# A first group's convolution ahead of the split and GpSimd work, the output projection's last weights in the decays' tiles, and Sqrt in a second norm

## The chip, the cores and the metric

The kernel runs on one core of a Trainium2 chip. The metric is the device time of one execution in microseconds. The program is one launch; three runs of the kernel before gave 746.96, 748.88 and 749.24 us, with a median of 748.88 us.

The core's engines are named as in the profile: PE (TensorE: matmuls and transposes), DVE (VectorE), ACT (ScalarE), POOL (GpSimd) and SP (SyncE, which issues the DMAs here). Each takes its own instructions in order; across engines they wait on semaphores.

## The reference

One sequence of 512 tokens with 1024 features goes through two layers and a norm, all in float32.

```python
def mamba2_layer(x, ...):
    h = rms_norm(x, norm_g)
    zxbcdt = h @ w_in
    # split into z, xbc, dt_raw
    xbc = silu(causal_depthwise_conv(xbc, conv_w, conv_b))      # 4 taps
    # xbc -> xs (heads), bm, cm (8 groups);  dt = softplus(...), a = -exp(a_log)
    y = ssd_chunked_scan(xs * dt[..., None], a * dt, bm, cm)
    y = y + d_skip * xs
    y = gated_group_rms_norm(y, z, gate_norm_g)                # norm of y * silu(z) per group
    return x + y @ w_out
...
x = mamba2_layer(x, ...)
k, v = shared_kv(x, kv_norm_g, w_kv)                           # own rms_norm, then x @ w_kv
x = diff_attention_layer(x, k, v, ...)                         # own rms_norm, queries and gate
return rms_norm(x, final_norm_g)
```

In the scan, with acs the running sum of a * dt within a chunk, position l sees position s of its chunk through exp(acs[l] - acs[s]) where s <= l and through zero elsewhere. This matrix is called the decay below. The two norms behind the first layer (for keys and values, and for the attention layer) divide by the same root, so the kernel computes it once; it is the second norm of the title. The sums of squares of a row's two halves go into it.

## The kernel before, in words

**Products.** Each float32 product is made of three matmuls (`mm3`): both factors are split into a rounded part and the rest, and hi*hi, hi*lo and lo*hi are summed. So each megabyte of weights (a segment) arrives by one DMA in a tile `raw`, and is split there by two operations for each slice k: `head` on ACT writes `whi`, `rest` on DVE writes `wlo` (`load`, `lay`). `raw`, `whi` and `wlo` have two buffers each. `use(seg)` fetches two segments ahead of the one that is used, and lays all pieces of a fetched segment in one go (`fetch`). From the last output projection on, `use_b` does it instead, and `paced` hands out the pieces one by one between the matmuls; `later(n, fn)` puts work off by n steps of that clock.

**The Mamba layer.** It has 8 groups, g0 to g7. The order of segments is written out by hand: z0 g0 g1 z1 g2 g3 z2 g4 o0 g5 z3 g6 g7 o1 o2 o3, each of two segments ("g",1,1 is the second one of g1, "o",3,1 the last one of the output projection), then v0 and the attention's. `group_proj(g)` projects into four PSUM banks pg and calls `conv` on each: u (DVE), Identity with the last tap (ACT), three taps by SCALAR_TENSOR_TENSOR (DVE), Silu (ACT). The results xc are B, C, x0 and x1 of the group. `z_proj` makes the gates zs by Silu from its banks pz, which are of the same four as pg.

`ssd(g)` is the scan of a group: pcb = B*C on PE, transposes pbt and pxt of B and x, xdt and dx from pxt (DVE), xe from xdt (POOL), dec * pcb (DVE), the states hst (psA, psB on PE, products on POOL, sums on DVE), pyd = dec times xdt on PE, po = C times the states, tmp from po; then gating, squares on ACT, a root on DVE (`rsqrt`, eight operations for one value), tmp scaled on ACT, its transposes pyt on PE, and yh and yl from these, which the output projection multiplies.

`decays(j)` (lines 497 to 515) makes the decay of groups 2j and 2j+1: a DMA brings acs into `dec` on all partitions (two buffers, so the DMA waits until the matmuls pyd of two groups before have read theirs), POOL copies `een` out, subtracts (TENSOR_TENSOR, four heads) and masks (AFFINE_SELECT), and ACT takes Exp of een and of dec in two halves. Exp and Silu each make ACT load another table (ACT_TABLE_LOAD), when the other was there before. `decays(0)` is called ahead of the groups, the next ones in `ssd` of g1, g3 and g5.

**Order.** Up to `last_rows` (line 637) a scheduler of the compiler sets the order of each engine. From `T.on = V.on = A.on = True` on, the order is that in which the program is written. All operations of DVE, ACT and PE go through the helper `Ordered` and so have its line, L53; the tiles tell them apart.

**The end of the Mamba layer.** `last_rows` multiplies by o31 (the weights of "o",3,1) and calls `row_norm(t, po)` for each of four blocks t of 128 tokens: after 1 step the add into x_tok (DVE), after 3 the square with its sum (ACT), after 6 the root (DVE: b_v, then seven operations of `rsqrt`), after 4 more the Copy with that scale into xn (ACT). `turn_rows` transposes xn (btp on PE) for the projections behind. Meanwhile v0's pieces are laid, one per two steps.

Of the kernel before, what the change touches and what calls it, by code (L numbers as in the profile page):

```python
# [9 lines left out]
F32 = mybir.dt.float32  # L10
F32R = mybir.dt.float32r
# [50 lines left out]
def trunk(ctx, tc, x, x_t, par, w_dt, w_in, w_out, w_kvqg, w_bo, d_skip, lam_qk, fin_g, out):  # L62
# [58 lines left out]
    def load(i):  # L121
# [8 lines left out]
        def split():  # L130
            hi = wp.tile([P, nk, w], F32R, tag="whi", name=f"whi{i}", bufs=2)
            lo = wp.tile([P, nk, w], F32R, tag="wlo", name=f"wlo{i}", bufs=2)
# [29 lines left out]

    def fetch(upto):
        while fetched[0] < min(upto, len(segs)):
            for piece in load(fetched[0])():
                lay(piece)
# [20 lines left out]
    def use_b(seg, first=None, pace=None):  # L187
# [3 lines left out]
        if i + 2 < len(segs) and fetched[0] == i + 2:  # L191
            loaded[i + 2] = load(i + 2)
        if i + 1 in loaded:
# [25 lines left out]
    def rsqrt(v, n, tag, bufs=2):  # L219
# [20 lines left out]
        return y  # L240

# [72 lines left out]
    conv_out = {}  # L314

# [122 lines left out]
    def conv(ps, ft, name, bufs):  # L438
# [5 lines left out]
        for k in (2, 1, 0):  # L444
            d = 3 - k
            V.scalar_tensor_tensor(out=xc[:, d:], in0=u[:, :S - d], scalar=cw[k], in1=xc[:, d:], op0=ALU.mult, op1=ALU.add)
# [3 lines left out]
    def group_proj(g):  # L450
# [14 lines left out]
        conv_out[g] = outs  # L465

# [30 lines left out]
    def decays(j):  # L497

        for g in (2 * j, 2 * j + 1):
            hs = slice(R * g, R * g + R)  # L500
            dec = bp.tile([P, R, NQ, P], F32, tag="dec", name=f"dec{g}", bufs=2)
            nc.sync.dma_start(dec.rearrange("p h c l -> p (h c l)"),
                                acs_d[hs].rearrange("h c l -> (h c l)").partition_broadcast(P))
            een = small.tile([P, R, 2], F32, tag="een", name=f"een{g}")
            GP.tensor_copy(een, dec[:, :, 1:3, P - 1])
            for h in range(R):
                GP.tensor_tensor(out=dec[:, h], in0=dec[:, h], in1=acs_tok[:, :, R * g + h].unsqueeze(2).to_broadcast([P, NQ, P]), op=ALU.subtract)  # L507
                GP.affine_select(out=dec[:, h], in_=dec[:, h], compare_op=ALU.is_ge, fill=-BIG, base=0,
                                 pattern=[[0, NQ], [1, P]], channel_multiplier=-1)
            decs[g] = (dec, een)  # L510
        for g in (2 * j, 2 * j + 1):
            dec, een = decs[g]
            A.activation(een, een, AF.Exp)
            for h in range(0, R, 2):
                A.activation(dec[:, h:h + 2], dec[:, h:h + 2], AF.Exp)
# [476 lines left out]
```

## Time and profile before

| what | us |
|---|---|
| median of three runs | 748.88 |
| the profiled execution's own time | 747.46 |
| its span, first to last instruction | 745.7 |
| PE busy | 723.1 |
| DVE busy | 553.5 |
| ACT busy | 437.9 |
| POOL busy | 132.3 |
| ACT_TABLE_LOAD, 27 of them | 34.6 |

A row of the timeline has the start in us from the span's beginning, the duration, the engine, the line, the operation, the tiles as output<-inputs, partitions x elements and types, how many like it were merged, and in brackets the idle time of the engine ahead of it with what ended it. The mean granted clock of PE is 0.993.

### The profile page before, as it was taken

What the parts mean: (1) busy time and instruction counts of PE and PEld (TensorE: products, weight loads), DVE (VectorE), ACT (ScalarE), POOL (GpSimd) and SP (SyncE); (2) the same over time, 40 slices, a digit from 0 to 9 for tenths busy, and PEclk for the clock granted to TensorE, in tenths of its full rate; (3) what the DMA queues carried; (4) which work ended last, traced back from release to release, by engine and by line L of the source; (5) the groups of instructions that cost most, each with busy time, mean ns of one, the idle gap of its engine ahead of it and who ended that gap; (6) DMA issues with size and microseconds to landing.
All of it is one profiled execution on the core that took longest, in us unless ns stands there. A gap on an engine that the chain in (4) does not pass through costs nothing.

```text
span 745.7 us, 10346 instructions
## 1 busy us (share of the span) xinstructions
PE 723.1 (97%) x3741; PEld 606.7 (81%) x3741; DVE 553.5 (74%) x1232; ACT 437.9 (59%) x951; POOL 132.3 (18%) x162
## 2 busy tenths in 40 slices
PE   9998999999999999998999998999999999999992
PEld 7786878888888888887888878888988898898881
DVE  5579994799679859667995648557767867885987
ACT  6837763574747428439542357657766766755535
POOL 0109261602515024150210110000000000000004
PEclk9999999999999999999999999999999999999997
DMA  9543223232213332221212111331221131131003
GB/s 317 204 150 136 96 75 114 69 125 89 113 57 113 120 125 74 95 96 62 108 62 109 57 57 65 113 113 57 65 106 56 58 114 57 58 114 57 29 1 113
DMA packets 12914, 70.83 MB, mean 95 GB/s; under 512 B 1600, under 2 KB 2112, under 8 KB 5312
## 3 DMA queue, kind: packets, MB, share of 16 engines
q1 hardware_dynamic: 12576, 70.06, 25.9%
q8 instruction: 29, 0.48, 0.3%
q10 hardware_dynamic: 288, 0.12, 0.1%
q14 instruction: 21, 0.17, 0.1%
HBM read 68.02 MB, written 2.16 MB: 94 GB/s over the span
## 4 chain that ended last, share of the span: by engine, by line
PE 81%; DVE 6%; ACT 5%; issue 4%; DMA 2%; POOL 0%; SPq 0%; ACTq 0%; POOLq 0%; DVEq 0%
PE pg L53 16%; PE po L53 14%; PE pz L53 9%; PE pt L53 7%; PE pq L53 6%; PE pk L53 6%; PE pv L53 6%; PE pb L53 5%; PE pyd L53 4%; PE sc L53 3%; DVE wlo L53 2%; ACT whi L53 1%; DVE xc L53 1%; DMA raw<-in_w_in 1%; PE psA L53 1%
## 5 line engine op out<-in xcount | busy, mean ns | idle before, releaser
L53 DVE SCALAR_TENSOR_TENSOR wlo<-raw,prm,whi 128x512 fp32r<-128x512 f32 (+1 forms) x256 | 155.6, 652 | 47.1 <-ACT whi L53 46.5
L53 ACT ACTIVATE whi<-raw,prm 128x512 fp32r<-128x512 f32 (+1 forms) x256 | 136.9, 604 | 46.0 <-PE po L53 14.4
L53 PE MATMUL pg<-a_hi,whi 128*128 128x512 f32 x256 | 102.8, 403 | 0.0
L53 PE MATMUL pg<-a_lo,whi 128*128 128x512 f32 x256 | 102.7, 401 | 0.0
L53 PE MATMUL pg<-a_hi,wlo 128*128 128x512 f32 x256 | 102.5, 401 | 0.0
L53 DVE SCALAR_TENSOR_TENSOR xc<-u,prm,xc 128x511 f32<-128x511 f32 (+2 forms) x96 | 79.7, 846 | 6.9 <-ACT xc L53 6.4
L53 PEld LDWEIGHTS pg<-a_hi,wlo 128*128 128x128 f32 x256 | 48.1, 188 | 10.9
L53 PEld LDWEIGHTS pg<-a_hi,whi 128*128 128x128 f32 x256 | 48.2, 188 | 10.9
L53 PEld LDWEIGHTS pg<-a_lo,whi 128*128 128x128 f32 x256 | 48.2, 188 | 10.5
L891 POOL TENSOR_TENSOR ot<-x_tok,fg 128x512 f32<-128x512 f32 x8 | 10.0, 1284 | 259.2 <-DVE x_tok L53 258.3
L53 PE MATMUL po<-whi,yh 128*128 128x512 f32 x128 | 51.3, 401 | 0.6 <-ACT yh L53 0.6
L53 PE MATMUL pz<-whi,a_lo 128*128 128x512 f32 x128 | 50.8, 397 | 0.0
L53 PE MATMUL po<-wlo,yh 128*128 128x512 f32 x128 | 50.7, 396 | 0.0
L53 PE MATMUL pz<-wlo,a_hi 128*128 128x512 f32 x128 | 50.6, 395 | 0.0
L53 PE MATMUL po<-whi,yl 128*128 128x512 f32 x128 | 50.3, 397 | 0.0
L53 PE MATMUL pz<-whi,a_hi 128*128 128x512 f32 x128 | 50.2, 404 | 0.0
L53 ACT ACTIVATE xc<-u,prm 128x512 f32<-128x512 f32 x32 | 25.8, 811 | 40.2 <-DVE u L53 40.1
L53 DVE CUSTOM_DVE_ANT_0 s<-sc,bias 128x128 f32<-128x128 f32 (+3 forms) x64 | 29.7, 486 | 22.7 <-PE sc L53 22.4
L545 POOL TENSOR_TENSOR xe<-xdt,tok 128x256 f32<-128x256 f32 x24 | 16.3, 707 | 149.1 <-DVE xdt L53 149.1
L507 POOL TENSOR_TENSOR dec<-dec,tok 128x512 f32<-128x512 f32 x32 | 40.5, 1296 | 0.6
L53 ACT ACT_TABLE_LOAD x27 | 34.6, 1283 | 9.2 <-DVE xc L53 6.3
L53 ACT ACTIVATE tmp<-dx 128x256 f32<-128x256 f32 x32 | 13.2, 412 | 45.1 <-DVE dx L53 45.1
(220 smaller groups left out, 1776.8 us busy)
## 6 DMA issues: line engine op xcount, KB each, us to landing
raw<-in_w_in SPq DMA_DIRECT2D x23, 1024.0 KB, 4.9
raw<-in_w_kvqg SPq DMA_DIRECT2D x16, 1024.0 KB, 4.8
dec<-acs_d SPq DMA_DIRECT2D x8, 1024.0 KB, 4.8
raw<-in_w_out SPq DMA_DIRECT2D x8, 1024.0 KB, 4.8
raw<-in_w_bo SPq DMA_DIRECT2D x4, 1024.0 KB, 4.9
xt<-in_x_t SPq DMA_DIRECT2D x8, 256.0 KB, 6.1
x_tok<-in_x SPq DMA_DIRECT2D x4, 512.0 KB, 8.7
out<-ot SPq DMA_DIRECT2D x8, 256.0 KB, 2.1
```

The lines of the kernel that those rows point to most:

```text
L53: i = op(*args, **kw)
L507: GP.tensor_tensor(out=dec[:, h], in0=dec[:, h], in1=acs_tok[:, :, R * g + h].unsqueeze(2).to_broadcast([P, NQ, P]), op=ALU.subtract)
L545: GP.tensor_tensor(out=xe[:, c], in0=xdt[:, c], in1=toe_tok[:, c, hs].unsqueeze(2).to_broadcast([P, R, HD]), op=ALU.mult)
L891: GP.tensor_tensor(out=ot[t][:, hs], in0=y, in1=fg[:, hs], op=ALU.mult)
```

## The change

There are three edits in one.

1. *First group.* The pieces of ("g",1,1) are held back in a list and laid after g0's convolutions; with `tc.issue_after` they may not stand ahead of the last tap. `decays` is cut into `decay_in` (the DMA), `decay_sub` (POOL) and `decay_exp` (ACT). At the start only group 0's decay is made whole, group 1 has its DMA alone; its subtractions follow POOL's operations of `ssd(0)`, and its Exp is written inside `ssd(0)`. Later decays are called as before, as `decays(g + 1, g + 2)`.
2. *Last weights.* The split of ("o",3,1) writes the two `dec` buffers instead of `whi` and `wlo`, and at `use_b(("o",3,0))` all of v0's pieces are laid at once.
3. *Roots.* `root1` makes a row's root by Sqrt on ACT and four small DVE operations (the negative value, a reciprocal, and one correction step), with other steps for `later`; the third `beside(8)` of the stretch is `beside(16)`.

```diff
         def split():
-            hi = wp.tile([P, nk, w], F32R, tag="whi", name=f"whi{i}", bufs=2)
-            lo = wp.tile([P, nk, w], F32R, tag="wlo", name=f"wlo{i}", bufs=2)
+
+            pool, tags = (bp, ("dec", "dec")) if seg == ("o", 3, 1) else (wp, ("whi", "wlo"))
+            hi, lo = (pool.tile([P, nk, w], F32R, tag=tag, name=f"{n}{i}", bufs=2) for n, tag in zip(("whi", "wlo"), tags))
             ready[seg] = (hi, lo)
...
 
+    held = []
+
     def fetch(upto):
         while fetched[0] < min(upto, len(segs)):
-            for piece in load(fetched[0])():
-                lay(piece)
+            held.extend(load(fetched[0])())
+            if segs[fetched[0] - 1] != ("g", 1, 1):
+                while held:
+                    lay(held.pop(0))
 
...
             loaded[i + 2] = load(i + 2)
+        if seg == ("o", 3, 0):
+            for piece in loaded.pop(i + 2)():
+                lay(piece)
         if i + 1 in loaded:
...
+
+    def root1(ss, vb, k, tag):
+
+        s, y, c, nv = (small.tile([P, 1], F32, tag=f"{tag}_{i}", name=f"{tag}_{i}", bufs=2) for i in "sycn")
+        A.activation(s, ss, AF.Sqrt, scale=k, bias=vb)
+
+        def rest():
+            V.tensor_scalar(out=nv, in0=ss, scalar1=-k, scalar2=vb, op0=ALU.mult, op1=ALU.subtract)
+            V.reciprocal(y, s)
+            V.tensor_scalar(out=c, in0=y, scalar1=nv, scalar2=y, op0=ALU.mult, op1=ALU.mult)
+            V.tensor_scalar(out=y, in0=c, scalar1=3.0, scalar2=y, op0=ALU.add, op1=ALU.mult)
+            return y
+
+        return rest
 
...
             d = 3 - k
-            V.scalar_tensor_tensor(out=xc[:, d:], in0=u[:, :S - d], scalar=cw[k], in1=xc[:, d:], op0=ALU.mult, op1=ALU.add)
+            conv_end[0] = V.scalar_tensor_tensor(out=xc[:, d:], in0=u[:, :S - d], scalar=cw[k], in1=xc[:, d:], op0=ALU.mult, op1=ALU.add)
         A.activation(xc, xc, AF.Silu)
...
 
+        if held:
+            with tc.issue_after(conv_end[0].ins):
+                while held:
+                    lay(held.pop(0))
+
...
 
-    def decays(j):
-
-        for g in (2 * j, 2 * j + 1):
-            hs = slice(R * g, R * g + R)
-            dec = bp.tile([P, R, NQ, P], F32, tag="dec", name=f"dec{g}", bufs=2)
-            nc.sync.dma_start(dec.rearrange("p h c l -> p (h c l)"),
-                                acs_d[hs].rearrange("h c l -> (h c l)").partition_broadcast(P))
-            een = small.tile([P, R, 2], F32, tag="een", name=f"een{g}")
+    def decay_in(g):
+
+        hs = slice(R * g, R * g + R)
+        dec = bp.tile([P, R, NQ, P], F32, tag="dec", name=f"dec{g}", bufs=2)
+        nc.sync.dma_start(dec.rearrange("p h c l -> p (h c l)"),
+                          acs_d[hs].rearrange("h c l -> (h c l)").partition_broadcast(P))
+        decs[g] = (dec, small.tile([P, R, 2], F32, tag="een", name=f"een{g}"))
+
+    def decay_sub(g, heads=range(R)):
+        dec, een = decs[g]
+        if 0 in heads:
             GP.tensor_copy(een, dec[:, :, 1:3, P - 1])
-            for h in range(R):
-                GP.tensor_tensor(out=dec[:, h], in0=dec[:, h], in1=acs_tok[:, :, R * g + h].unsqueeze(2).to_broadcast([P, NQ, P]), op=ALU.subtract)
-                GP.affine_select(out=dec[:, h], in_=dec[:, h], compare_op=ALU.is_ge, fill=-BIG, base=0,
-                                 pattern=[[0, NQ], [1, P]], channel_multiplier=-1)
-            decs[g] = (dec, een)
-        for g in (2 * j, 2 * j + 1):
-            dec, een = decs[g]
-            A.activation(een, een, AF.Exp)
-            for h in range(0, R, 2):
-                A.activation(dec[:, h:h + 2], dec[:, h:h + 2], AF.Exp)
+        for h in heads:
+            GP.tensor_tensor(out=dec[:, h], in0=dec[:, h], in1=acs_tok[:, :, R * g + h].unsqueeze(2).to_broadcast([P, NQ, P]), op=ALU.subtract)
+            GP.affine_select(out=dec[:, h], in_=dec[:, h], compare_op=ALU.is_ge, fill=-BIG, base=0,
+                             pattern=[[0, NQ], [1, P]], channel_multiplier=-1)
+
+    def decay_exp(g):
+        dec, een = decs[g]
+        A.activation(een, een, AF.Exp)
+        for h in range(0, R, 2):
+            A.activation(dec[:, h:h + 2], dec[:, h:h + 2], AF.Exp)
+
+    def decays(*gs):
+        for g in gs:
+            decay_in(g)
+            decay_sub(g)
+        for g in gs:
+            decay_exp(g)
+
+    def behind(g, i, heads):
+        if g == 0:
+            with tc.issue_after(i.ins):
+                decay_sub(1, heads)
 
...
         for c in range(3):
-            GP.tensor_tensor(out=xe[:, c], in0=xdt[:, c], in1=toe_tok[:, c, hs].unsqueeze(2).to_broadcast([P, R, HD]), op=ALU.mult)
+            xe_end = GP.tensor_tensor(out=xe[:, c], in0=xdt[:, c], in1=toe_tok[:, c, hs].unsqueeze(2).to_broadcast([P, R, HD]), op=ALU.mult)
+
+        behind(g, xe_end, (0,))
         for h in range(R):
...
         A.copy(hsf[:, 0], psA[:, 0:256])
-        GP.tensor_tensor(out=hst[:, 1], in0=hst[:, 0], in1=een[:, :, 0:1].to_broadcast([P, R, HD]), op=ALU.mult)
+        i = GP.tensor_tensor(out=hst[:, 1], in0=hst[:, 0], in1=een[:, :, 0:1].to_broadcast([P, R, HD]), op=ALU.mult)
+        behind(g, i, (1,))
         V.tensor_tensor(out=hsf[:, 1], in0=psA[:, 256:512], in1=hsf[:, 1], op=ALU.add)
         psB = ss_bank(f"psB{g}")
         T.matmul(psB[:, 0:256], lhsT=bt[:, 2, :], rhs=xe[:, 2].rearrange("p h e -> p (h e)"), start=True, stop=True)
-        GP.tensor_tensor(out=hst[:, 2], in0=hst[:, 1], in1=een[:, :, 1:2].to_broadcast([P, R, HD]), op=ALU.mult)
+        i = GP.tensor_tensor(out=hst[:, 2], in0=hst[:, 1], in1=een[:, :, 1:2].to_broadcast([P, R, HD]), op=ALU.mult)
+        behind(g, i, (2, 3))
+        if g == 0:
+            decay_exp(1)
         V.tensor_tensor(out=hsf[:, 2], in0=psB[:, 0:256], in1=hsf[:, 2], op=ALU.add)
...
         if g % 2 and g < G - 1:
-            decays((g + 1) // 2)
+            decays(g + 1, g + 2)
 
...
     decays(0)
+    decay_in(1)
     dense[0] = stream_a()
...
-
-        def root():
-            v = small.tile([P, 1], F32, tag="f_v", name=f"b_v{t}", bufs=2)
-            V.scalar_tensor_tensor(out=v, in0=bss[:, 1, t:t + 1], scalar=ROOT2 / D, in1=bss[:, 0, t:t + 1], op0=ALU.mult, op1=ALU.add)
-            r = rsqrt(v, 1, "f")
-            later(4, lambda: A.activation(xn[t], x_tok[:, t], AF.Copy, scale=r))
+            rest = root1(bss[:, 1, t:t + 1], bss[:, 0, t:t + 1], 4.0 / D, "b")
+            later(3, lambda: root(rest))
+
+        def root(rest):
+            r = rest()
+            later(2, lambda: A.activation(xn[t], x_tok[:, t], AF.Copy, scale=r))
 
         later(1, lambda: V.tensor_tensor(out=y, in0=po, in1=y, op=ALU.add))
         later(3, square)
-        later(6, root)
 
...
     T.on = V.on = A.on = True
-    later(9, lambda: V.tensor_scalar(out=bss[:, 0], in0=bss[:, 0], scalar1=ROOT2 / D, scalar2=ROOT2 * EPS, op0=ALU.mult, op1=ALU.add))
+    later(9, lambda: V.tensor_scalar(out=bss[:, 0], in0=bss[:, 0], scalar1=4.0 / D, scalar2=4.0 * EPS, op0=ALU.mult, op1=ALU.add))
     dense[0] = paced(last_rows())
...
     turn_rows("b", 3, xn[3], hh, hl)
-    beside(8)
+    beside(16)
     flush()
```

**Where the orders differ.** The orders of PE, ACT, DVE and POOL differ from g0's convolutions up to about g3 and again from o3 on; in between they are the same, and SP's is the same throughout. ACT has 36 table loads instead of 27.

First DVE at the end of g0's convolutions, before; xc_614 is x0, xc_634 x1, u their scaled input, wlo_553 the second segment of g1, dec_440 group 0's decay:

```order
L53 SCALAR_TENSOR_TENSOR xc_614<-u_615,prm,xc_614 128x511
L53 TENSOR_TENSOR u_635<-pg_3_489,ar_row 128x512
L53 SCALAR_TENSOR_TENSOR wlo_553<-raw_550,prm,whi_552 128x512
L53 SCALAR_TENSOR_TENSOR xc_614<-u_615,prm,xc_614 128x510
L53 SCALAR_TENSOR_TENSOR wlo_553<-raw_550,prm,whi_552 128x512 x3
L53 SCALAR_TENSOR_TENSOR xc_614<-u_615,prm,xc_614 128x509
L53 SCALAR_TENSOR_TENSOR xc_634<-u_635,prm,xc_634 128x511
L53 SCALAR_TENSOR_TENSOR xc_634<-u_635,prm,xc_634 128x510
L53 SCALAR_TENSOR_TENSOR xc_634<-u_635,prm,xc_634 128x509
L53 TENSOR_TENSOR dec_440<-dec_440,pcb_661 128x512 x4
```

The same place now, where the names are xc_586 and xc_606 and wlo_533:

```order
L53 SCALAR_TENSOR_TENSOR xc_586<-u_587,prm,xc_586 128x511
L53 TENSOR_TENSOR u_607<-pg_3_469,ar_row 128x512
L53 SCALAR_TENSOR_TENSOR xc_586<-u_587,prm,xc_586 128x510
L53 SCALAR_TENSOR_TENSOR xc_586<-u_587,prm,xc_586 128x509
L53 SCALAR_TENSOR_TENSOR xc_606<-u_607,prm,xc_606 128x511
L53 SCALAR_TENSOR_TENSOR xc_606<-u_607,prm,xc_606 128x510
L53 SCALAR_TENSOR_TENSOR xc_606<-u_607,prm,xc_606 128x509
L53 SCALAR_TENSOR_TENSOR wlo_533<-raw_530,prm,whi_532 128x512 x4
```

The four wlo have moved from between the taps of x0 to behind those of x1.

Next ACT at the convolutions of g1, before; xc_850 is B and xc_870 C of g1, and TABLE_LOAD stands wherever Exp and Silu alternate:

```order
L53 COPY hst_696<-psA_697 128x256
L53 ACT_TABLE_LOAD
L53 ACTIVATE xc_850<-xc_850 128x512
L53 ACTIVATE xc_870<-xc_870 128x512
L53 ACTIVATE tmp_708,ss_707<-dx_673 128x256
L53 ACTIVATE xc_890<-u_891,prm 128x512
L53 ACTIVATE whi_828<-raw_826,prm 128x512 x4
```

The same place now; dec_463 is group 1's decay:

```order
L53 COPY hst_681<-psA_682 128x256
L53 ACT_TABLE_LOAD
L53 ACTIVATE xc_850<-xc_850 128x512
L53 ACT_TABLE_LOAD
L53 ACTIVATE dec_463<-dec_463 128x1024
L53 ACT_TABLE_LOAD
L53 ACTIVATE xc_870<-xc_870 128x512
L53 ACTIVATE xc_890<-u_891,prm 128x512
L53 ACTIVATE tmp_708,ss_707<-dx_653 128x256
L53 ACTIVATE whi_828<-raw_826,prm 128x512 x4
```

A dec Exp with a table load on either side now stands between the Silu of B and that of C; the second half of it comes behind the four whi that follow.

Last ACT in `ssd(1)`, before; zs_2 and zs_3 are gates of z1, which read the banks pz_2 and pz_3, xc_1304 and xc_1324 are B and C of g2, een_1027 belongs to group 3's decay:

```order
L53 ACTIVATE tmp_984,ss_983<-dx_949 128x256
L53 ACTIVATE zs_2_1200<-pz_2_920,ar_col 128x512
L53 ACTIVATE tmp_984,ss_983<-dx_949 128x256
L53 ACTIVATE zs_3_1214<-pz_3_921,ar_col 128x512
L53 ACTIVATE tmp_984,ss_983<-dx_949 128x256
L53 ACTIVATE whi_1222<-raw_1220,prm 128x512 x4
L53 ACTIVATE tmp_984,ss_983<-dx_949 128x256
L53 ACT_TABLE_LOAD
L53 ACTIVATE een_1027<-een_1027 128x8
L53 ACTIVATE xc_1324<-u_1325,prm 128x512
```

The same place now:

```order
L53 ACTIVATE tmp_984,ss_983<-dx_949 128x256
L53 ACTIVATE zs_2_1200<-pz_2_920,ar_col 128x512
L53 ACTIVATE xc_1304<-u_1305,prm 128x512
L53 ACTIVATE xc_1324<-u_1325,prm 128x512
L53 ACTIVATE xc_1304<-xc_1304 128x512
L53 ACT_TABLE_LOAD
L53 ACTIVATE een_1027<-een_1027 128x8
L53 ACTIVATE tmp_984,ss_983<-dx_949 128x256
L53 ACT_TABLE_LOAD
L53 ACTIVATE zs_3_1214<-pz_3_921,ar_col 128x512
L53 ACTIVATE xc_1324<-xc_1324 128x512
```

een_1027 and two table loads have moved from behind zs_3 to ahead of it. On PE, pg_3 of g2, which takes the bank of pz_3, comes at this place behind pyd_1 and po of g1 and the first twelve matmuls of pg_2; before, those of pg_2 came ahead of pyd_1.

1 line of the change is left out of this document (added).

## The prediction

> **What bounds the kernel now.** The page first.
>
> ```profile
> span 745.7 us, 10346 instructions
> ...
> PE 723.1 (97%) x3741; PEld 606.7 (81%) x3741; DVE 553.5 (74%) x1232; ACT 437.9 (59%) x951; POOL 132.3 (18%) x162
> ...
> L53 ACT ACT_TABLE_LOAD x27 | 34.6, 1283 | 9.2 <-DVE xc L53 6.3
> ```
>
> TensorE (PE) is busy for 97% of the span and takes its instructions in a fixed order, so a change can win only time in which PE waits, and it loses every wait that it opens. So the timeline of PE comes second: its matmuls of 128x512 start about 0.23 us apart, and I look for larger steps. These are the ones that the change aims at, with the two matmuls ahead of the first.
>
> ```profile
> 67.67 0.40 PE L53 MATMUL pg<-a_hi,wlo 128*128 128x512 f32 x1
> 67.91 0.40 PE L53 MATMUL pg<-a_hi,whi 128*128 128x512 f32 x1
> 70.94 0.66 PE L53 MATMUL pxt<-ident,xc 128*128 128x128 f32 x4 [2.63 <-ACT xc L53]
> ...
> 73.60 0.66 PE L53 MATMUL pxt<-ident,xc 128*128 128x128 f32 x4 [0.16 <-ACT xc L53]
> ...
> 450.54 1.09 PE L53 MATMUL btp<-ident,xn 128*128 128x128 f32 x8 [1.27 <-ACT xn L53]
> ...
> 458.98 1.09 PE L53 MATMUL btp<-ident,xn 128*128 128x128 f32 x8 [0.73 <-ACT xn L53]
> ```
>
> From start to start less 0.23, the wait at 70.94 costs 2.80 us, 0.17 more than the idle time that the row names. With as much for the others they cost 0.33 (73.60), 1.44 (450.54) and 0.90 (458.98). So at most 3.1 us can be won in the first group and 2.3 at the second norm. Everything else is what the new orders of ACT, DVE and POOL cost.
>
> **Part 1: g0's convolution ahead of the held split.** The timelines of DVE, ACT and POOL in front of the wait at 70.94:
>
> ```profile
> 63.16 0.74 DVE L53 SCALAR_TENSOR_TENSOR xc<-u,prm,xc 128x510 f32<-128x510 f32 x1
> 63.82 3.61 DVE L53 SCALAR_TENSOR_TENSOR wlo<-raw,prm,whi 128x512 fp32r<-128x512 f32 x3
> 67.35 5.47 DVE L53 SCALAR_TENSOR_TENSOR xc<-u,prm,xc 128x509 f32<-128x509 f32 x4
> ...
> 65.52 1.06 ACT L53 ACTIVATE dec<-dec 128x1024 f32<-128x1024 f32 x1
> 68.96 1.28 ACT L53 ACT_TABLE_LOAD   x1 [2.39 <-DVE xc L53]
> 70.25 0.63 ACT L53 ACTIVATE xc<-xc 128x512 f32<-128x512 f32 x1
> ...
> 65.40 5.84 POOL L507 TENSOR_TENSOR dec<-dec,tok 128x512 f32<-128x512 f32 x4
> ```
>
> Three wlo operations (3.6 us) stand between the second and the third tap of x0, and the taps beside POOL's subtractions take 1.37 us each where one alone took 0.74. Without both, x0's taps end near 64.5, and ACT becomes the late one: its second dec exponential ends at 66.58, then the table load (1.28) and Silu (0.63), so xc is there at 68.5. PE's new order comes to pxt one matmul earlier, at 67.9. The wait shrinks from 2.80 to 0.65 and that at 73.60 goes: **-2.5 us** (bounds -3.1, no wait left, to -2.0, with taps still slowed).
>
> **Part 2: decay 1 inside ssd(0), wait A.** In before, all of group 1's decay was done while PE had slack; now ACT does it between the convolutions of g1. In the new order the Silu of xc_870, which pcb of g1 reads, stands behind TABLE_LOAD, Silu, TABLE_LOAD, dec exp, TABLE_LOAD.
>
> ```profile
> 82.46 3.22 DVE L53 SCALAR_TENSOR_TENSOR xc<-u,prm,xc 128x511 f32<-128x511 f32 x4 [0.28 <-ACT xc L53]
> ...
> 85.75 1.28 ACT L53 ACT_TABLE_LOAD   x1 [2.37 <-DVE xc L53]
> 87.05 0.63 ACT L53 ACTIVATE xc<-xc 128x512 f32<-128x512 f32 x1
> ...
> 92.15 1.05 PE L53 MATMUL pcb<-xc,xc 128*128 128x128 f32 x8
> ```
>
> In before the chain starts when the fourth tap ends, 85.68. Now: 2.5 earlier, one tap more in front (0.8), and some 1.3 of slowing beside POOL's subtraction (two taps at 1.37 for 0.74): 85.3. Then 1.28 + 0.63 + 1.28 + 1.06 + 1.28 + 0.63 = 6.2, so xc_870 is there at 91.5. PE comes to pcb at 92.15 - 2.5 + 0.23 (one matmul later in its order) = 89.9. **A = +1.6** (0.2 without slowing, 2.0 with the full 85.7). SP's order is unchanged. On POOL the subtractions for group 1 now stand between xe and the products for the states; I cost that at nothing, since PE has both pyd ahead of the po that reads the states; with that cover gone one subtraction (5.84 / 4 = 1.5) is late there.
>
> By the Trainium skill ("ScalarE: Activation LUTs", What ACT_TABLE_LOAD costs) a switch of sets takes the 1283 ns load and a drain of about 1380 ns, 2.66 us, and its Table sets section says to group calls by set, which speaks against this order; A would then be 1.6 + 3 x 1.38 = 5.7. The trace shows the load's 1.28 and no drain behind it: 85.75 + 1.28 = 87.03, and Silu starts at 87.05.
>
> **Wait B: pyt of g0.** PE's new order puts these transposes seven 128x512 matmuls (1.63 us) earlier, while ACT's chain to tmp has three extra table loads, a split dec exponential and waits for DVE's four dec products.
>
> ```profile
> 72.74 2.47 DVE L53 TENSOR_TENSOR dec<-dec,pcb 128x512 f32<-128x512 f32 x4
> ...
> 89.23 0.81 ACT L53 ACTIVATE xc<-u,prm 128x512 f32<-128x512 f32 x1
> 89.95 2.55 ACT L53 ACTIVATE whi<-raw,prm 128x512 fp32r<-128x512 f32 x4
> ...
> 110.62 1.69 ACT L53 ACTIVATE tmp<-dx,y_y 128x256 f32<-128x256 f32 x4
> ...
> 143.05 0.19 ACT L53 ACTIVATION_READ_ACCUMULATOR tmp<-dx 128x1 f32 x1
> 143.26 1.28 ACT L53 ACT_TABLE_LOAD   x1
> 144.55 0.21 ACT L53 ACTIVATE een<-een 128x8 f32<-128x8 f32 x1
> ...
> 111.24 1.56 PE L53 MATMUL pyt<-ident,tmp 128*128 128x128 f32 x8
> ```
>
> ACT from 91.5: ident 0.8, square 0.6 (0.42 as for tmp, and the accumulator's 0.19), whi x4 2.55, load 1.28, exp 1.06, ident 0.8: 98.6. DVE then: a tap 0.7, dec x4 2.5, another tap 0.7, and three gate products of some 0.4: 103.7, up to 105.2 if POOL's next subtractions slow them. Then ACT: last square 0.6, load 1.28, Silu 0.63, load 1.28, exp 1.06, one whi 0.64, tmp 0.42: 109.6 to 111.1; I take 111.0, since POOL's subtractions do run there. PE, 0.9 ahead after A, arrives at 111.24 - 1.63 - 0.9 = 108.7. The wait is 2.3, and the next three tmp follow at 0.42, a little slower than their transposes: **B = +2.5** (0.4 to 4).
>
> **Wait C: pg_3 of g2.** The new ACT order puts zs_3, which empties the PSUM bank that pg_3 needs, behind een_1027's exponential. That waits for POOL's copy, and that for the reload of dec, which starts when pyd_1 of g1 has read the old one. PE's new order has po, twelve matmuls of pg_2, then pg_3.
>
> ```profile
> 135.69 1.51 PE L53 MATMUL po<-hst,xc 128*128 128x256 f32 x6
> 136.85 0.58 PE L53 MATMUL pg<-a_hi,whi 128*128 128x512 f32 x1
> ...
> 140.70 0.19 POOL L505 COPY een<-dec 128x8 f32<-128x8 f32 x1 [1.14 <-DMA dec<-acs_d]
> ...
> 138.71 0.67 ACT L53 ACTIVATE zs<-pz,ar_col 128x512 f32<-128x512 f32 x1
> ```
>
> In before zs (138.71) went ahead of the copy (140.70) and nobody waited. From the end of pyd_1, both sides: the reload 5.0 (135.69 to 140.70), copy 0.3, exp 0.2, a square 0.6, load 1.3, zs 0.7: 8.1; PE: po 1.2, twelve matmuls 2.8: 4.0. **C = +4.0** (3.5 to 4.5), the surest term, since both sides start from one event. After it the order of all engines is that of before up to g7.
>
> **Part 3: the end.** o31's weights go to dec tiles, v0 is split at once, and its wlo leave DVE's stretch after 443.
>
> ```profile
> 427.70 2.56 ACT L53 ACTIVATE whi<-raw,prm 128x512 fp32r<-128x512 f32 x4 [2.10 <-issue]
> 430.17 1.70 ACT L53 ACTIVATE tmp<-dx,y_y 128x256 f32<-128x256 f32 x4
> ...
> 433.05 1.04 PE L53 MATMUL pyt<-ident,tmp 128*128 128x128 f32 x8
> ...
> 443.27 0.40 PE L53 MATMUL po<-whi,yl 128*128 128x512 f32 x1
> ...
> 443.61 1.69 DVE L53 SCALAR_TENSOR_TENSOR wlo<-raw,prm,whi 128x256 fp32r<-128x256 f32 x4 [1.27 <-ACT whi L53]
> 445.29 0.69 DVE L53 TENSOR_TENSOR x_tok<-po,x_tok 128x512 f32<-128x512 f32 x1
> ...
> 446.07 0.63 ACT L53 ACTIVATE xn<-x_tok 128x512 f32<-128x512 f32 x1 [0.89 <-DVE x_tok L53]
> ...
> 449.34 1.15 ACT L53 ACTIVATE xn<-x_tok,f_y 128x1024 f32<-128x1024 f32 x1 [1.35 <-DVE f_y L53]
> ```
>
> PE ends the first po of o31 at 443.67; the add waits behind wlo to 445.29. Now it goes at 443.7: add 0.7, square 0.8, Sqrt's table load 1.3, Sqrt 0.2 (een's row), three small DVE operations 0.6, Copy 1.15: 448.5, before PE's 449.1. Behind the wlo, as the add stands now, the load would make it late. PE's order in this stretch and the work that it does are unchanged, so the new paces cost nothing by themselves. Both waits go: **-2.3** (-1.0 if it covers only the first in part). Before that, v0's eight whi of half the width (3.4 us, an estimate: two thirds of the 0.64 of a whole one) stand where o31's four (2.56) stood, and the last steps of y's root stand between v0's wlo: tmp starts near 432.2 for 430.2, its fourth is there near 433.9, where PE's last pair stands at 433.65: **+0.3** (0 to 0.9).
>
> **Sum** against the profiled execution's own 747.46 (span 745.7): -2.5 + 1.6 + 2.5 + 4.0 - 2.3 + 0.3 = +3.6, so 751.1. The median of the runs shown is 748.88, 1.4 above that execution: **752.5**. The bounds together (a smaller gain in part 1 also lets PE arrive later at A) are -1.3 to +8.4; two at an end at once are unlikely, so the forecast's own range is 748 to 756.
>
> **Rivals.**
> (1) Faster: A, B and C do not open, because ACT (59% busy) takes the extra loads in its idle time and PE's order gives it room. For it: ACT idles 2.37 at 85.75. Against: that idle lies ahead of the chain, not in it. Point of decision: een_1027's copy landing within 4 us of pyd_1's end, where before's row shows 5.0. 748.88 - 2.5 - 2.0 = **744.4**.
> (2) No difference: only C, or only A with B, is there: -4.5 with +4.0 or +4.1 gives **748.4**. For it: A's and B's lower ends are 0.2 and 0.4.
> (3) Slower still: the cover at the end is gone (the add doesn't get ahead, Sqrt's load is on the path), so 1.3 of the 2.3 stays lost, and B at its upper end: 752.5 + 1.3 + 1.5 = **755.3**.
> (4) The skill's drain, with A at 5.7: its rule would give 752.5 + 4.1 = 756.6. The rows 143.05 (ends 143.24) and 143.26 show no drain in front of a load either, so I give it 1 in 50.
>
> **How the numbers follow.** Forecast 0.53, rival 1 0.20, rival 2 0.19, rivals 3 and 4 together 0.08. A measurement of this kernel tells about 0.3% (2.25 us) from no change, so faster is below 746.6 and slower above 751.1. Of the forecast's own spread a fifth (0.10) lies in the band, and of rival 2 a small part on either side: faster 0.21, same 0.25, slower 0.54. For 8 in 10 the range takes in half of rival 1: 744.5 to 756.
>
> **What would show it.** In the profile of after: pxt of g0 near 68.5 with a wait under 1 us (part 1); waits named ACT xc at pcb of g1 near 91.5, ACT tmp at pyt of g0 near 111, and ACT zs at pg of about 4 us some 4 us behind pyd (A, B, C); no wait at btp; 36 table loads of 1.28. I am wrong if PE's sum of waits between 60 and 150 us is below 5 us, and above all if no wait for zs stands there.

## The result, and the profile after

The changed kernel takes 752.89 us (median of six runs, 751.86 to 754.38) where the kernel before takes 749.16 (six runs, 746.96 to 749.66). The ratio is 1.0059, with a 95% interval of 1.0047 to 1.0072: slower by 0.6% (the two medians alone give 1.0050). The profiled execution is the one of 751.86 us. Its page:

```profile
span 750.1 us, 10342 instructions
...
PE 726.3 (97%) x3741; PEld 608.2 (81%) x3741; DVE 553.9 (74%) x1216; ACT 449.2 (60%) x964; POOL 128.7 (17%) x162
...
PEclk9999998999999999999999999999999999999996
...
L53 ACT ACT_TABLE_LOAD x36 | 46.2, 1283 | 15.0 <-DVE xc L53 6.5
```

The span grew by 4.4 us (745.7 to 750.1). ACT is busy for 11.3 us more; the nine added table loads alone are 11.6. One thing on this page stood in no step of the prediction: the seventh slice of PEclk (112 to 131 us) has an 8 where before had nines.

PE's timeline at the places that the prediction named:

```profile
68.11 0.66 PE L53 MATMUL pxt<-ident,xc 128*128 128x128 f32 x4
...
90.76 1.16 PE L53 MATMUL pcb<-xc,xc 128*128 128x128 f32 x8 [1.18 <-ACT xc L53]
...
112.12 1.97 PE L53 MATMUL pyt<-ident,tmp 128*128 128x128 f32 x8 [3.86 <-ACT tmp L53]
...
114.38 0.78 PE L53 MATMUL pz<-whi,a_lo 128*128 128x512 f32 x1
114.96 0.63 PE L53 MATMUL pz<-whi,a_hi 128*128 128x512 f32 x1
115.38 0.63 PE L53 MATMUL pz<-wlo,a_hi 128*128 128x512 f32 x1
...
141.92 0.40 PE L53 MATMUL pg<-a_hi,whi 128*128 128x512 f32 x1
...
154.53 0.50 PE L53 MATMUL pg<-a_hi,wlo 128*128 128x512 f32 x1 [0.36 <-DVE wlo L53]
...
160.81 1.64 PE L53 MATMUL pyt<-ident,tmp 128*128 128x128 f32 x8 [0.41 <-ACT tmp L53]
...
456.02 1.03 PE L53 MATMUL btp<-ident,xn 128*128 128x128 f32 x8
```

The waits at pxt and at btp are gone, those at pcb and at pyt of g0 are there, and no wait stands at 141.92, where the dearest one was forecast. In its place PE runs at half pace for a while (starts 0.42 to 0.43 apart instead of 0.23 from 114.96 on, five times), and two small waits stand at the end of g1.

A ledger puts sizes on these. For each event I take its start less what the matmuls ahead of it cost at an even pace, in both traces; the difference shows where time is won and lost although PE's order changed.

| stretch | difference so far | step | forecast |
|---|---|---|---|
| up to psA of g0 (part 1) | -2.96 | -2.96 | -2.5 |
| up to pcb of g1 (wait A) | -1.62 | +1.34 | +1.6 |
| up to pyt of g0 (wait B) | +2.51 | +4.13 | +2.5 |
| up to pxt of g1 (half pace) | +4.42 | +1.91 | none |
| up to pcb of g2 (wait C) | +4.42 | 0.0 | +4.0 |
| up to pxt of g2 (end of g1) | +6.49 | +2.07 | none |
| up to pyt of g7 (v0's split) | +6.53 | +0.04 | +0.3 |
| to the end (both waits at btp) | +4.4 | -2.1 | -2.3 |

Four steps came out near their forecast, and B 1.6 above it. Wait C, the largest loss of the sum, did not happen, and losses that the sum did not have filled its place. The row of v0's split covers all from g2 on; from pxt to pyt of g7 alone the difference is +0.22, where the forecast's +0.3 belongs.

### The profile page after: what moved, and what is told of

Its sections match the earlier page's. It is cut to its first block, busy times and chain, and to the rows that moved or that the text cites. A ratio compares the mean times of both kernels' runs of the same rounds, so it can differ in the third digit from the quotient of the medians.

```text
span 750.1 us, 10342 instructions
## 1 busy us (share of the span) xinstructions
PE 726.3 (97%) x3741; PEld 608.2 (81%) x3741; DVE 553.9 (74%) x1216; ACT 449.2 (60%) x964; POOL 128.7 (17%) x162
## 4 chain that ended last, share of the span: by engine, by line
PE 75%; DVE 8%; ACT 8%; issue 5%; DMA 2%; POOL 0%; SPq 0%; ACTq 0%; POOLq 0%; DVEq 0%
PE po L53 15%; PE pg L53 12%; PE pt L53 7%; PE pz L53 7%; PE pq L53 6%; PE pv L53 6%; PE pk L53 6%; PE pb L53 5%; PE pyd L53 3%; PE sc L53 3%; DVE wlo L53 2%; ACT L53 2%; ACT whi L53 2%; DVE xc L53 1%; ACT xc L53 1%
## 5 line engine op out<-in xcount | busy, mean ns | idle before, releaser
L53 DVE SCALAR_TENSOR_TENSOR wlo<-raw,prm,whi 128x512 fp32r<-128x512 f32 (+1 forms) x256 | 150.1, 631 | 39.1 <-ACT whi L53 38.7
L53 ACT ACTIVATE s<-s,mx 128x128 f32<-128x128 f32 (+3 forms) x64 | 35.6, 558 | 4.2 <-DVE mx L53 4.1
```

The lines of the kernel that those rows point to most:

```text
L53: i = op(*args, **kw)
```

## The experiments

All are variants of the changed kernel. "Alone" means that the other edits are put back as they were before. The runs of before that ran beside them had medians of 748.68 (first to fourth), 748.90 (fifth to eighth) and 748.49 us (the last four). Single executions also start differently: pcb of g0, ahead of which PE does the same 223 projection matmuls in all kernels, stands between 65.1 and 66.2 us, so a time in one profile compares with one in another only to about 1 us.

**1. The first edit alone.** The second and third edits are put back:

```diff
-            pool, tags = (bp, ("dec", "dec")) if seg == ("o", 3, 1) else (wp, ("whi", "wlo"))
+            pool, tags = wp, ("whi", "wlo")
...
-            rest = root1(bss[:, 1, t:t + 1], bss[:, 0, t:t + 1], 4.0 / D, "b")
+            r = rsqrt(v, 1, "f")
```

> The first group's edit alone (held split, decay 1 moved into the first scan); weights' tiles and root as before. Theory 1, the loss is the first group's: PE's waits at pcb of g1 (about 1.4 us), at pyt of g0 (about 4, with some 1.5 of slow matmuls behind it) and at g1's end (about 2) stand here without the end's gain, so 6.3 us slower than before, 755.5. Rival, the loss comes from the end (table load of Sqrt, decays' tiles) or from nowhere in particular: within 1 us of before.

Measured: 754.63 us (754.13 to 755.66), ratio 1.0078 (1.0065 to 1.0091). The profile has the waits of the full change at nearly the same places (1.17 at pcb of g1, 3.86 at pyt of g0 with five slow matmuls behind it, 0.41 and 0.42 at the end of g1) and those of 1.27 and 0.73 at btp as in before. The whole loss is the first edit's.

**2. The second and third edits alone.** `held` and the split of `decays` are put back:

```diff
-    decays(0)
-    decay_in(1)
+    decays(0, 1)
...
-            if segs[fetched[0] - 1] != ("g", 1, 1):
+            if True:
```

> The end's two edits alone (last weights in the decays' tiles, Sqrt); the first group as before. Theory 1: both waits at btp go, about 0.2 comes at pyt of g7, so 2.1 us faster than before, 747.1. Rival: no faster, 749 or more.

Measured: 747.78 us (745.64 to 750.06), ratio 0.9988 (0.9977 to 1.0000). The waits at btp are gone. The median gains 0.9 where the ledger has 2.1. Its profiled run lost about 1.0 of that elsewhere: behind the wait of 2.63 us at g0's pxt, which before has as well, four matmuls start at half pace (72.6 to 73.9). That is the granted clock, shown below; over all its executions the mean clock was 0.990, over those of before beside it 0.992.

**3. The hold alone.** Only the pieces of ("g",1,1) are held; both decays are made at the start, so `decays(0, 1)` stands again.

> Only the held split; the decays are all made at the start as before. Theory 1 (the price is the table loads and waits of decay 1's Exp between the convolutions of g1): pxt of g0 comes 2 to 2.6 us earlier, no wait at pcb of g1; the scheduler's order has 31 table loads here for 27, so a part of the wait at pyt of g0 may come; 746.5 to 748.5. Rival (the price is the held split itself, whose wlo come late for g1's projection): a wait for wlo on PE behind pxt, and 750 or more.

Measured: 751.02 us (748.78 to 752.20), ratio 1.0027 (1.0016 to 1.0037): a little slower, where theory had it faster. The wait at pxt does go. But POOL still subtracts and masks group 1 at 65.5 to 75.1, beside DVE's held pieces:

```profile
69.92 4.65 DVE L53 SCALAR_TENSOR_TENSOR wlo<-raw,prm,whi 128x512 fp32r<-128x512 f32 x4
...
76.88 0.68 DVE L53 TENSOR_TENSOR xdt<-pxt,tok 128x512 f32<-128x512 f32 x1
```

In the changed kernel the same four pieces take 2.73 (from 67.06), and xdt starts at 72.10. Here DVE is 4.8 later (1.0 of it is the later start of this execution), xe is late with it, and new waits stand at psA and psB (0.42 and 0.32, for xe), and at pyt of g0 (1.62 at 114.1). The hold alone moves the lateness from pxt to what follows; POOL's work has to go too for part 1's gain.

**4. The decay's move alone.** Only `decay_sub` and `decay_exp` of group 1 are inside `ssd(0)`; the pieces are not held.

> Only the moved decay 1; the split of g1's second segment is not held. Theory 1: the taps of x0 are no longer slowed but still stand behind the wlo, so at most 1.5 us of the first wait goes; waits at pcb of g1 and pyt of g0 come as in the full change: 752 to 756. Rival (the price is the held split): 748 or less.

Measured: 750.82 us (748.57 to 751.93), ratio 1.0024 (1.0012 to 1.0036). That is less than theory had, which also had a wait at pcb of g1. The wait at pxt falls from 2.63 to 1.37, none stands at pcb of g1, and that at pyt of g0 is 2.46. ACT's chain between the two Silus is there with all three table loads (84.08 to 90.32), but PE comes to pcb at 91.25 only. So wait A needs both halves of the edit: PE must come early (hold) and Silu be late (Exp between the convolutions).

**5. The full change with decay 1's Exp behind the last Silu of g1.** This is the test of A and B: the subtractions stay where the change put them, ACT's Exp alone is moved.

```diff
-        if g == 0:
-            decay_exp(1)
...
         until(f"g{g}")
+        if g == 1:
+            with tc.issue_after(silu_end[0].ins):
+                decay_exp(1)
         ssd(g)
```

> The full change, but with the Exp of group 1's decay issued on ACT behind the last Silu of g1's convolutions (it is needed only for dec times pcb of g1), so without table loads between these Silus. Theory 1 (the loss is the Exp's place, with its table loads, between the convolutions): no wait at pcb of g1, the wait at pyt of g0 under 2 us and no slow matmuls behind it; with both gains kept 743.5 to 746. Rival (PE's new order, which comes to pcb and pyt earlier, is the cause): waits of 1 us and more stay at both, 750 or more.

Measured: **745.35 us** (743.78 to 746.53), ratio 0.9961 (0.9950 to 0.9973). It beats the kernel before and, by about 1%, the changed one. Its timelines of ACT and PE:

```profile
84.63 0.63 ACT L53 ACTIVATE xc<-xc 128x512 f32<-128x512 f32 x1 [4.13 <-DVE xc L53]
85.62 0.63 ACT L53 ACTIVATE xc<-xc 128x512 f32<-128x512 f32 x1 [0.36 <-DVE xc L53]
...
112.91 1.70 ACT L53 ACTIVATE tmp<-dx,y_y 128x256 f32<-128x256 f32 x4
```

```profile
113.47 1.63 PE L53 MATMUL pyt<-ident,tmp 128*128 128x128 f32 x8 [1.30 <-ACT tmp L53]
```

Two Silus follow each other with no table load between them, and wait A is gone. Wait B is 1.30 instead of 3.86, but not because tmp came sooner: it comes at 112.91, later than the 111.58 of the changed kernel. Counting the matmuls of pz, pg and po ahead of pyt gives 384 in this kernel and 362 in the changed one. The scheduler put 22 more (22 x 0.233 = 5.1 us) in front of the transposes. Behind a wait of 1.30 there is no half pace, and the end of g1 has no waits. The kernel has 28 table loads.

**6. The next decays issued behind POOL's dx sums.** In `ssd` of g1, g3 and g5 the call of `decays` is tied behind the last sum. It asks whether een's copy, which waits for its DMA in front of these sums, causes the waits at the end of g1.

```diff
-        if g % 2 and g < G - 1:
-            decays(g + 1, g + 2)
...
+        if g % 2 and g < G - 1:
+            with tc.issue_after(dx_end.ins):
+                decays(g + 1, g + 2)
```

> The full change, but in every second scan the next decays' work on POOL (and with it their Exp on ACT) is queued behind the three dx sums. That takes group 2's Exp out of ACT's chain to tmp of g0 and een's copy out from between g1's dx sums; group 1's Exp stays between the convolutions. Theory 1: the wait at pcb of g1 stays at 1.4; that at pyt of g0 falls by the Exp and its table load, 2.3, to under 2, without slow matmuls; the waits at the end of g1 (1.1 us) go: 747 to 749.5. Rival (POOL slowing DVE, not ACT's chain, makes the wait at pyt): the wait stays at 4, 751.5 or more.

Measured: 764.2 us (762.87 to 764.63), ratio 1.0209 (1.0189 to 1.0229). A miss in the time: the decays behind g1 now come late, the order of all groups changes, and new waits stand at 148.5 (2.52), 167.4 (2.19) and 265.1 (4.61). On the end of g1 it says nothing clean, since waits of its own stand there. But it settles wait B. The wait at pcb of g1 is 1.18, as in the changed kernel, and 361 matmuls stand ahead of pyt of g0 (362 there). ACT's and PE's rows at that place:

```profile
107.22 1.71 ACT L53 ACTIVATE tmp<-dx,y_y 128x256 f32<-128x256 f32 x4 [0.63 <-DVE y_y L53]
...
109.33 1.04 PE L53 MATMUL pyt<-ident,tmp 128*128 128x128 f32 x8
```

Group 2's subtractions (POOL's four at 100.48 in the changed kernel) and its Exp (ACT's of een at 100.60 and of dec at 110.00) are no longer there; tmp comes 4.4 us sooner and nobody waits. DVE is undisturbed there; the two products from 103.85 are those from 103.20 in the changed kernel (2.46):

```profile
103.85 0.75 DVE L53 TENSOR_TENSOR dx<-dx,zs 128x256 f32<-128x256 f32 x2
```

**7. PE kept busy in front of pyt of g0.** Four matmuls of 512 columns, whose result is overwritten, fill the wait; the theory was that they cost their own time and take the half pace away.

```diff
+            if g == 0 and j == 0:
+                for n in range(4):
+                    T.matmul(pyt, lhsT=ident, rhs=dx[:, 2:4]..., start=True, stop=True)
```

> The full change, with four matmuls of 128x512 more, whose result is overwritten by pyt of g0: they stand some twelve matmuls ahead of it and use up the time in which PE only waits for tmp. Theory 1 (the 0.43 us matmuls behind the wait come from PE having been idle for 3.9 us): no slow matmuls, 1.3 to 1.5 us faster than the full change, 751.4. Rival (they come from something else at that place): slow matmuls stay, 753 or more.

Measured: 763.1 us (760.2 to 764.57), ratio 1.0193 (1.0163 to 1.0223). Also a miss, and inconclusive. The four wait themselves (2.21 at 106.2, for DVE's dx) and take 5.4 us, since now they run at half pace (granted clock 0.5 from 106.9 to 110.3); the matmuls behind pyt do start 0.23 apart, and the scheduler answers the new instructions with another order that has waits of 3.11 at 155.1 and 3.58 at 219.7.

**8. The hold with the second and third edits.** Both decays at the start again, all else as in the change.

> The full change without the moved decay 1: held split, decays' tiles, Sqrt. Theory 1, parts add: the held split alone took 2.3 us more than before and the end alone 0.9 less, so 749 to 751. Rival (the held split's waits and the end's gain depend on each other): 747 or less.

Measured: 748.14 us (747.08 to 751.50), ratio 0.9996 (0.9983 to 1.0009). The waits of the hold alone (0.42, 0.32, 1.61) are there, those at btp are gone. The sum of the parts was 749 to 751, so this is a little below it, and above the rival's 747: no change in all.

**9. The third edit alone,** the root by Sqrt, with o31's split in whi and wlo as in before.

> The kernel before with the third edit alone (the Sqrt root and its paces); the last weights stay in whi and wlo. Theory 1 (what keeps PE waiting at btp is that the first add stands behind o31's wlo on DVE): the add still ends near 446.0, and then square 0.8, Sqrt's table load 1.3, Sqrt 0.2, three small DVE operations 0.6 make 448.9 where the Copy starts at 449.34 in before, so at most 0.4 is won: 748.5, between 747.9 and 749.5, and a wait of 0.8 to 1.3 is still named at the first btp. Rival (the eight small operations of the old root are what is late): both waits at btp go, 747.0 or less.

Measured: 749.9 us (748.76 to 754.0), ratio 1.0024 (1.0011 to 1.0037): not faster but slower. The timelines of DVE, ACT and PE behind the same add:

```profile
447.61 0.68 DVE L53 TENSOR_TENSOR x_tok<-po,x_tok 128x512 f32<-128x512 f32 x1
...
449.13 1.28 ACT L53 ACT_TABLE_LOAD   x1
452.83 1.15 ACT L53 ACTIVATE xn<-x_tok,b_y 128x1024 f32<-128x1024 f32 x1 [0.91 <-DVE b_y L53]
...
454.03 1.36 PE L53 MATMUL btp<-ident,xn 128*128 128x128 f32 x8 [2.44 <-ACT xn L53]
```

From the add's start to the Copy's start it takes 452.83 - 447.61 = 5.2 us; in before it is 449.34 - 445.29 = 4.05. The table load, and two wlo that come between b_s and the small operations, make the first wait 2.44 instead of 1.27; the later waits go, since the load comes once. By the ledger the waits at btp together cost only 0.2 more than in before (+1.17 at the first, -1.00 at the third); the rest of the loss in this stretch, 1.5, is half pace behind the wait of 2.44.

**10. The second edit alone,** o31's split in the dec tiles, the root as in before.

> The kernel before with the second edit alone (o31's weights in the dec tiles, v0 laid at once); the old root stays. Theory 1: the add goes at 443.7 instead of 445.3, the Copy 1.6 earlier, so the wait of 1.27 at the first btp goes and that of 0.73 too; with 0.2 to 0.3 lost at g7's transposes that gives 747.0, between 746.5 and 747.8. Rival (the root is what is late): a wait at btp stays above 0.7 and the time is 748.5 to 749.2.

Measured: 747.01 us (745.84 to 748.87), ratio 0.9979 (0.9969 to 0.9989). PE's timeline at the first btp:

```profile
451.22 1.09 PE L53 MATMUL btp<-ident,xn 128*128 128x128 f32 x8 [0.20 <-ACT xn L53]
```

1.27 became 0.20, and no wait stands at the later ones. The second edit carries the gain of the end. What Sqrt adds to it is this last wait of 0.20; the medians of the two together (0.9988) and of this one (0.9979) don't differ by more than their intervals.

**11. As the fifth, without the hold.**

> The kernel with decay 1's Exp behind g1's last Silu, but with the second segment of g1 split at once again (hold undone). Theory 1 (in that kernel the hold still wins what the decay alone leaves open, a wait of 1.37 at g0's pxt against 0.2): 1.2 to 1.6 slower than that kernel, 746.5 to 747.0. Rival (the hold on its own loses, as the hold alone did by 2 us, and only the late Exp wins): 743.0 to 745.0.

Measured: 751.25 us (750.48 to 752.44), ratio 1.0043 (1.0030 to 1.0056). Both theories miss: taking the hold away costs 5.9 us here. PE's timeline shows where:

```profile
111.68 1.97 PE L53 MATMUL pyt<-ident,tmp 128*128 128x128 f32 x8 [4.34 <-ACT tmp L53]
```

The wait at pxt is small (0.58 at 69.1) without the hold too. But 360 matmuls stand ahead of pyt of g0, 24 fewer than in the fifth, and the wait is 4.34 with half pace behind it. By the ledger this trace ends 6.7 us behind that of the fifth: 0.8 of it arises at pxt, 4.1 at pyt of g0 and in the half pace behind it, the rest from g2 on (waits of 0.49 and 0.71 at pxt of g2 and g4). That the hold "wins" 5.9 us in this company and lost 2 alone is for the larger part the scheduler's placing of pyt, not its effect on DVE.

**12. As the fifth, without the second and third edits.**

> The first edit alone, with decay 1's Exp behind g1's last Silu; the last weights and the root as in before. Theory 1 (parts add up: the end is worth 1.1 by its own run and 2.1 by the lag of the two traces): 745.35 plus 1.1 to 2.1, so 746.5 to 747.5, with waits of 1.3 and 0.7 at btp and none above 0.3 at the end of g1. Rival (the end is worth nothing once the front is smooth): 745.0 to 746.0.

Measured: 747.27 us (745.92 to 748.47), ratio 0.9983 (0.9972 to 0.9993), 1.9 us above the fifth. The front and the end add up: waits of 1.28 and 0.73 at btp, 1.24 at pyt of g0 (384 matmuls ahead of it again), none above 0.3 at the end of g1.

## Why the prediction was right or wrong

The sign and the size came out (752.5 forecast, 752.89 measured), but not by the whole sum, and that they agree to 0.4 us is luck. Wait C's 4.0 never came; B's excess (1.6), the half pace (1.9) and the end of g1 (2.1) filled its place, and part 1, A and v0's split came out 1.0 lower together. By its own signs the prediction failed where it was surest: no wait for zs stands there, and the waits named between 60 and 150 us come to 5.04 us (1.18 + 3.86), hardly above the 5 that it set.

**Part 1, right.** With the hold, DVE goes through the taps in one piece, and ACT becomes the late one, as forecast. The timelines of DVE and ACT:

```profile
64.82 2.32 DVE L53 SCALAR_TENSOR_TENSOR xc<-u,prm,xc 128x511 f32<-128x511 f32 x3 [0.93 <-ACT xc L53]
67.06 2.73 DVE L53 SCALAR_TENSOR_TENSOR wlo<-raw,prm,whi 128x512 fp32r<-128x512 f32 x4
...
66.12 1.28 ACT L53 ACT_TABLE_LOAD   x1
67.42 1.15 ACT L53 ACTIVATE xc<-xc 128x512 f32<-128x512 f32 x2
```

Silu starts at 67.42 where 67.86 was reckoned (66.58 + 1.28), so 0.23 of excess is left at pxt instead of 0.65, and the gain is 2.96 instead of 2.5.

**Wait A, right.** ACT's chain in front of pcb of g1 is the one forecast, instruction for instruction:

```profile
84.47 1.28 ACT L53 ACT_TABLE_LOAD   x1 [4.12 <-DVE xc L53]
85.77 0.63 ACT L53 ACTIVATE xc<-xc 128x512 f32<-128x512 f32 x1
86.42 1.28 ACT L53 ACT_TABLE_LOAD   x1
87.71 1.06 ACT L53 ACTIVATE dec<-dec 128x1024 f32<-128x1024 f32 x1
88.79 1.28 ACT L53 ACT_TABLE_LOAD   x1
90.08 0.63 ACT L53 ACTIVATE xc<-xc 128x512 f32<-128x512 f32 x1
```

It starts 0.8 sooner than reckoned (85.3) and PE too comes a little sooner, so +1.34 for +1.6. The rows answer the rival of the drain as well: loads start 0.01 to 0.02 us behind the instruction ahead of them (85.77 + 0.63 = 86.40, load at 86.42). The fifth and the fourth experiment show the cause, though each changed the order as well: without Exp between the Silus, or without PE's early arrival, the wait isn't there.

**Wait B, right in kind, too small.** +4.13 came for +2.5, just above the upper bound of 4. Rows of DVE, POOL and ACT:

```profile
101.74 1.53 DVE L53 SCALAR_TENSOR_TENSOR xc<-u,prm,xc 128x510 f32<-128x510 f32 x1
103.20 2.46 DVE L53 TENSOR_TENSOR dx<-dx,zs 128x256 f32<-128x256 f32 x2
105.58 1.11 DVE L53 SCALAR_TENSOR_TENSOR xc<-u,prm,xc 128x509 f32<-128x509 f32 x1
...
100.48 4.89 POOL L538 TENSOR_TENSOR dec<-dec,tok 128x512 f32<-128x512 f32 x4
...
104.50 0.42 ACT L53 ACTIVATE tmp<-dx 128x256 f32<-128x256 f32 x1 [2.14 <-DVE dx L53]
...
106.77 1.28 ACT L53 ACT_TABLE_LOAD   x1 [0.57 <-DVE xc L53]
...
108.71 1.28 ACT L53 ACT_TABLE_LOAD   x1
110.00 1.06 ACT L53 ACTIVATE dec<-dec 128x1024 f32<-128x1024 f32 x1
...
111.58 1.69 ACT L53 ACTIVATE tmp<-dx,y_y 128x256 f32<-128x256 f32 x4
```

The gate products dx beside POOL's subtractions take 1.23 us each where some 0.4 was taken, and a tap 1.53 for 0.74, so ACT waits 2.14 for the second product. tmp starts at 111.58 for a forecast end of its first at 111.0 (range 109.6 to 111.1): the upper end was too low by about 0.9, and PE came at 108.3 rather than 108.7. The mis-sized term is that of DVE's slowing: the step took the gate products at their undisturbed 0.4, and raised the range for slowing by 1.5 in all, where the second dx alone waited 2.14. The sixth experiment shows that this work of the next decay is the cause: with it out of the way the wait is gone, at the same place in PE's order. From the end of the first gate product to the start of tmp the changed kernel takes 9.8 us (101.82 to 111.58) and the sixth 4.0 (103.26 to 107.22). Of the difference, 2.4 lie ahead of the end of the last square, where DVE is slowed (the step had 1.4 for that), and 3.4 behind it, where the table loads and Exp stand, which the step had.

**Wait C, wrong.** The chain that the step followed ran as forecast. The timelines of ACT and POOL:

```profile
135.01 0.67 ACT L53 ACTIVATE zs<-pz,ar_col 128x512 f32<-128x512 f32 x1
...
142.80 0.21 ACT L53 ACTIVATE een<-een 128x8 f32<-128x8 f32 x1
...
143.42 1.28 ACT L53 ACT_TABLE_LOAD   x1
144.72 0.69 ACT L53 ACTIVATE zs<-pz,ar_col 128x512 f32<-128x512 f32 x1
...
140.05 1.18 POOL L639 TENSOR_TENSOR dx<-dx,tmp 128x256 f32<-128x256 f32 x1 [7.07 <-DVE tmp L53]
142.50 0.26 POOL L536 COPY een<-dec 128x8 f32<-128x8 f32 x1 [1.27 <-DMA dec<-acs_d]
142.73 1.94 POOL L639 TENSOR_TENSOR dx<-dx,tmp 128x256 f32<-128x256 f32 x2
```

zs_3 ends at 145.4, 7.6 us behind the end of pyd_1 for the 8.1 reckoned, and pg_3 starts at 141.92 all the same. The step failed where it said that zs_3 "empties the PSUM bank that pg_3 needs". In the built program, of both kernels, pg_3 of g2 has the bank of pz_2, whose zs ended at 135.7; the bank of pz_3 goes to a projection of g3. So what the text on the change says of pg_3's bank is wrong too. I took the banks of pg and pz to pair up by number, and looked at neither kernel's addresses. The "surest term" was sure of its times and not of its reader.

**The end of g1, not foreseen.** een's copy was followed to ACT, and not to what stands behind it on POOL: two of three dx sums wait with it (142.73) for the DMA. In the fifth experiment the three sums run from 140.48 ahead of the copy, and the waits at the end of g1 are gone. That fits, but it isn't shown: 515 matmuls stand ahead of pyt of g1 in the changed kernel, 541 in before and 548 in the fifth, so PE also comes there earlier than it did, by 26 x 0.233 = 6.1 us of work. Counted from po of g1, the first tmp is there after 23.0 us in the changed kernel, 24.2 in before and 20.4 in the fifth, and PE's own work up to the transposes takes some 21.9, 25.3 and 23.0. Against before it is therefore PE's earlier arrival that opens the wait at pyt, for tmp comes no later; against the fifth, tmp is 2.6 late, and the last dx sum 1.9 (6.2 behind po for 4.3). That the copy alone makes this lateness no run shows. The two waits are 1.1 of the 2.07; most of the rest is the eight transposes, which follow tmp one by one.

**The half pace, not foreseen.** +1.9 behind wait B; more below.

**The end, right in the sum and half right in its reason.** -2.1 for -2.3, by the wlo leaving the add's way (tenth experiment). The prediction's remark that "behind the wlo, as the add stands now, the load would make it late" is what the ninth measured: 5.2 us from add to Copy for 4.05.

**The rivals.** The first (no waits in g1 because ACT has room) was wrong for this order, but near what the fifth experiment reaches with Exp moved and another order: 745.35 for its 744.4. The point of decision that it named, een_1027's copy within 4 us of pyd's end, decided nothing: the copy came 4.7 behind it (142.50), and C had no reader.

## What to carry to other kernels

An Exp put between Silus costs two table loads on that engine's chain, and costs them on PE as soon as PE comes early: with the Exp moved behind the last Silu the kernel went from 0.6% slower to 0.4% faster, though much of that came by the order that the scheduler then made. Before a buffer's late release is priced as a wait, look up who has that buffer in the built program; a chain worked out to 0.3 us is worth nothing without its reader. Where a scheduler sets the order, a variant that moves one instruction moves the whole order, so compare how much work stands ahead of the waiting matmul (384 against 360 here) before a gain or a loss is put down to the edit. And price a wait of PE of some 2 us or more with the half pace that can follow it.

## What the runs showed of the hardware

A long wait of PE costs more than itself. The windows of the granted clock in the changed kernel, around its wait of 3.86 us (the figure ahead of the last two is PEclk):

```profile
108.20:112.20 4.00, 0.14 (x2) 0.08 (x2) 1.82 (x9) 3.97 (x6) 0.16 (x1) 0.78 0.00 0
112.00:118.00 6.00, 5.88 (x21) 4.92 (x22) 2.53 (x4) 5.97 (x11) 0.00 (x0) 0.56 0.18 26
```

In the kernel before, and in the one with the second and third edits alone, PE waits 2.63 us at g0's pxt. Here is that place in before:

```profile
71.00:75.00 4.00, 3.84 (x20) 3.00 (x21) 3.96 (x6) 2.06 (x3) 3.49 (x5) 1.00 0.14 57
```

and in the other:

```profile
71.00:75.00 4.00, 3.70 (x12) 3.09 (x13) 3.96 (x6) 1.95 (x3) 3.85 (x5) 0.58 0.25 107
```

The same wait, with a clock of 1.00 behind it in one execution and 0.58 in the other, 20 matmuls in four microseconds against 12. Over the fourteen profiles of this case, all seven waits of 3.09 us and more were followed by half the clock; of eight waits from 2.19 to 2.63 five were, and of twelve waits of 1.94 to 1.97 at g6's pcb four.

The times at which the traces record a change of the clock show what decides. In each trace all of them lie on a grid of 3.41 us that runs through the whole execution and lies differently in each; so the stretches of half clock last 3.41 us (13 of 16) or 6.83 (three). All 16 waits of which 1.96 us or more fell between two points of the grid were followed by such a stretch, and none of the 28 others of 1.17 us and more, of which 1.61 at most fell there. In before, the 2.63 us were cut into 1.29 and 1.35; in the other, into 2.25 and 0.39. The wait of 3.86 us was cut into 2.17 and 1.69, and half clock lasted from 110.4 to 117.3. By the Trainium skill ("TensorE: Matmul & The Clock Gate", Part 1, What's actually happening) the clock falls to half after an idle window of about 3.4 us, and the window runs free of the kernel. The grid agrees with that length and with a free-running window; but the window need not be idle throughout, as 1.96 us of its 3.41 were enough here.

By the ledger such a stretch costs 1.6 us behind g6's pcb (in all four profiles that have it) and 1.9 behind wait B, and nothing in the next execution. It makes a good part of the 2 to 4 us by which single executions of one kernel differ: the 70 executions of before that ran beside the experiments took 747.6 us on average where the mean clock was 0.993 or more (15 of them), 748.9 at 0.991 or 0.992 (51) and 750.3 at 0.988 or 0.989 (4), and one stretch of 3.41 us at half clock is 0.0023 of the mean. All six executions of the changed kernel had 0.988 or 0.990.
